# A gated decoder layer: the gates' sigmoids and VectorE's step on them, issued one product later and pinned in their queues

## The chip, the core and the metric

The kernel runs on one core of a Trainium2 chip. The metric is device time in microseconds (us) of one execution. The engines named below are TensorE (PE; its weight loads are listed as PEld), VectorE (DVE), ScalarE (ACT), GpSimd (POOL) and SyncE (SP), which issues most of the DMA transfers. SBUF is the on-chip memory, PSUM the banks into which TensorE accumulates.

## The reference

One layer of a decoder with two token mixers in parallel, a sequence of 2048 positions, width 1024, all in float32. What matters here:

```
h = u @ w_in            # u: the modulated input, 2048 x 1024
q, k, v, a_gate, p_in, p_gate, m_a, m_p = split(h)
a = attention(q, k, v) * silu(a_gate);                     a = a @ w_attn_proj
p = (pool(p_in) @ w_pool_mix * pool_scale) * silu(p_gate); p = p @ w_pool_proj
y = sigmoid(m_a) * a + sigmoid(m_p) * p
...                     # y @ w_out, gate, layer norm
```

Four of the eight parts of h are gates, 1024 wide each. All four go through a sigmoid; `a_gate` is multiplied with its sigmoid (silu), `p_gate` with its sigmoid and with `pool_scale`, and `m_a` and `m_p` stay plain sigmoids.

## The kernel before

**Products.** A float32 product is made of three matmuls on high and low parts (`mm3`). Each weight tile must therefore be split first: ScalarE casts it to its high part (`a.copy(by_two(hi), raw)`, L311) and VectorE subtracts that from the tile to get the low part (`low`, L128). For the last quarter of the weights the cast is L318. The names for the outcome of both are `w_set`.

The products are arranged in a scheme with seven products where eight would be needed (Strassen's). A `Quad` stands for two weight tiles by two column halves, so for four output blocks of 128 x 512. Its seven products are called, by the set of inputs that they use, B11 and T1 (in `front`) and T2, B21, T3, B22, T4 (in `back`). Each product is 12 matmuls of 128 x 512. The sums of weights that a quad needs are formed on GpSimd (L279, L283, L284, L289), some additions on results too (L362, of `p5`).

A result comes free in this order, and `q.consume` is called on each:

- (0, 0): PSUM bank `a`, after B21, with no addition;
- (1, 1): `p5`, after T3 and an addition on VectorE (L378);
- (0, 1): `c12`, after B22 and an addition (L386);
- (1, 0): `u2`, after T4 and an addition (L406).

`ring` runs the quads in groups of two (one group has one): for both quads T2 and B21, then T3 and B22 of the first, T3 and B22 of the second, T4 of both, then B11 and T1 of the next group's quads.

**Gates.** `gate_quads(s)` lists for one half `s` of the sequence one quad for keys and values and 16 gate quads, in nine groups. The first half's phase (`first_phase`) runs from about 75 to 460 us and the second half's (`second_phase`) from about 760 to 1080 us. Between them and after them lie attention, and at the end projections and the norm. A gate block is 128 x 512: a sigmoid on ScalarE (L516), for half of the gates one step on VectorE (L518 for silu, L520 with `pool_scale`), and a store of 256 KB to memory. In all there are 128 sigmoids, 64 steps and 128 stores.

**What sets the order.** Instructions written through `nc.scalar`, `nc.vector` and so on are put into their engine's queue by a scheduler, which may move them. Those written through the wrappers `act`, `dve`, `pe`, `pool`, `sp` (class `Ordered`) are pinned: they keep the order of the program among themselves. TensorE's are all pinned. `tick()` is called after each product. It runs what is hooked at that place (loads and splits of other data sets, pooled weights), counts up, and runs what is due: `defer(n, f)` puts `f` down for the n-th `tick` from now. The store of a gate is deferred by 2.

**Work beside the gates.** Hooks in the two phases prepare data for later stages: sums of inputs and their high and low parts (`k_hi` on ScalarE, `k_lo` on VectorE, stored from there), folds of pooled weights (`mr`, `mhi`, `mlo`), and loads. The transposed weights that are folded with these come through `spare`.

**Buffers.** The sigmoid's tile comes from a pool of five buffers with tag "c", shared with `c12`, `k_hi`, `k_lo`, `vt`, `mr`, `st_hi` and `st_lo`; whoever takes a buffer waits for the one before to be done with it, the landing of its store included. `u2` and `p5` share four buffers with tag "p". PSUM banks with tag "mm" are four.

Of the kernel before, what the change touches and what calls it, by code (L numbers as in the profile page):

```python
# [13 lines left out]
AF = mybir.ActivationFunctionType  # L14
ALU = mybir.AluOpType
# [43 lines left out]
def kernel(  # L59
# [22 lines left out]
    nc = tc.nc  # L82
    pe, act, dve, pool, sp = (Ordered(tc, e) for e in (nc.tensor, nc.scalar, nc.vector, nc.gpsimd, nc.sync))
# [13 lines left out]
    psc = cp.tile([P, KT], F32, name="psc")  # L97
# [23 lines left out]
    gates_d = {n: dp.tile([2, KT, 2, P, CH], F32, name=f"{n}_d") for n in ("ag", "pg", "ma", "mp")}  # L121
# [289 lines left out]
    def defer(ticks, f):  # L411
        due.append((now[0] + ticks, len(due), f))
# [99 lines left out]

    def gate_quad(s, name, base, m, kind):
        def consume(ph, mi, t, src):
            g = ph.c("sig")
            nc.scalar.activation(g, src, AF.Sigmoid)  # L516
            if kind == "silu":
                nc.vector.tensor_tensor(g, g, src, ALU.mult)  # L518
            elif kind == "scaled":
                nc.vector.scalar_tensor_tensor(g, src, psc[:, m + mi : m + mi + 1], g, ALU.mult, ALU.mult)  # L520
            defer(2, lambda: sp.dma_start(gates_d[name][s, m + mi, t], g))

        return Quad((win[base + m], win[base + m + 1]), consume)

# [847 lines left out]
```

## Time and profile before

| what | us |
|---|---|
| three runs | 1878.24, 1870.00, 1867.99 |
| median | 1870.0 |
| profiled execution | 1861.84 |
| its span in the profile | 1860.1 |
| TensorE busy in the span | 1735.2 |
| VectorE busy | 1315.5 |
| ScalarE busy | 938.5 |
| GpSimd busy | 935.5 |

The profiled execution is a fourth one; its own time is 1.7 us above its span. Rows of the profile give an engine, the line of the program that issued the work, the operation and its tiles (out<-in, by the names in the program). In the timeline a row begins with its start and its length in us, and ends in brackets with the idle time of the engine before it and with what ended that. Rows of waits give the engine and line that waited, what it waited for, the total in us, the count and the longest. Rows of a tile's view give the shortest, median and longest duration in ns, then the first and last start in us.

### The profile page before, as it was taken

What the parts mean: (1) busy time and instruction counts of PE and PEld (TensorE: products, weight loads), DVE (VectorE), ACT (ScalarE), POOL (GpSimd) and SP (SyncE); (2) the same over time, 40 slices, a digit from 0 to 9 for tenths busy, and PEclk for the clock granted to TensorE, in tenths of its full rate; (3) what the DMA queues carried; (4) which work ended last, traced back from release to release, by engine and by line L of the source; (5) the groups of instructions that cost most, each with busy time, mean ns of one, the idle gap of its engine ahead of it and who ended that gap; (6) DMA issues with size and microseconds to landing.
All of it is one profiled execution on the core that took longest, in us unless ns stands there. A gap on an engine that the chain in (4) does not pass through costs nothing. (4 is left out here: it accounts for less than half of the span.)

```text
span 1860.1 us, 25320 instructions
## 1 busy us (share of the span) xinstructions
PE 1735.2 (93%) x8248; PEld 1436.4 (77%) x8248; DVE 1315.5 (71%) x2284; ACT 938.5 (50%) x1977; POOL 935.5 (50%) x758
## 2 busy tenths in 40 slices
PE   6689899989999999999999999999989989999996
PEld 6467777777888888787777788888867778777775
DVE  5776766544677787777666457777857887886886
ACT  3543434333777776544444457777724333422453
POOL 0454445433254677545445314556763785476543
PEclk9889999999999999999999999999999999999998
DMA  9245566766344447785777733544786574689432
GB/s 346 74 163 189 198 218 213 254 211 180 107 144 163 159 154 294 262 285 196 254 258 251 259 126 120 181 145 139 278 300 204 185 258 155 214 291 382 146 140 104
DMA packets 163571, 381.32 MB, mean 205 GB/s; under 512 B 19680, under 2 KB 23792, under 8 KB 163440
## 3 DMA queue, kind: packets, MB, share of 16 engines
q1 hardware_dynamic: 150560, 342.95, 52.9%
q0 software_dynamic: 10112, 33.06, 5.2%
q10 hardware_dynamic: 2768, 3.70, 0.9%
q8 instruction: 65, 1.06, 0.2%
q14 instruction: 66, 0.54, 0.1%
HBM read 244.35 MB, written 138.44 MB: 206 GB/s over the span
## 5 line engine op out<-in xcount | busy, mean ns | idle before, releaser
L55 PE MATMUL mm<-set_B,w_set 128*128 128x512 f32 x3240 | 804.1, 396 | 31.7 <-DVE w_set L128 24.3
L55 PEld LDWEIGHTS mm<-set_B,w_set 128*128 128x128 f32 x3240 | 602.2, 189 | 165.8 <-DVE w_set L128 33.5
L55 PE MATMUL lg<-set_T,w_set 128*128 128x512 f32 x2088 | 529.1, 403 | 61.9 <-ACT w_set L311 24.6
L55 PEld LDWEIGHTS lg<-set_T,w_set 128*128 128x128 f32 x2088 | 398.6, 193 | 168.9 <-ACT w_set L311 33.2
L128 DVE TENSOR_TENSOR w_set<-W,w_set 128x1024 fp32r<-128x1024 f32 x162 | 241.4, 1490 | 142.4 <-ACT w_set L311 137.2
L311 ACT CAST w_set<-W 128x1024 fp32r<-128x1024 f32 x162 | 169.3, 1049 | 239.0 <-PE mm L55 146.8
L55 PE MATMUL mm<-set_T,w_set 128*128 128x512 f32 x1080 | 269.0, 397 | 0.6 <-ACT set_T L55 0.3
L55 PEld LDWEIGHTS mm<-set_T,w_set 128*128 128x128 f32 x1080 | 202.3, 190 | 44.6 <-ACT set_T L55 1.5
L289 POOL TENSOR_TENSOR W<-W 128x512 f32<-128x512 f32 x56 | 81.3, 1451 | 158.5 <-DVE w_set L128 149.4
L283 POOL TENSOR_TENSOR W<-W 128x512 f32<-128x512 f32 x56 | 86.8, 1550 | 130.8 <-DVE w_set L128 114.4
L362 POOL TENSOR_TENSOR p<-p,u 128x512 f32<-128x512 f32 x58 | 98.8, 1705 | 104.5 <-DVE u L361 102.2
L55 DVE TENSOR_TENSOR o<-pv,o 64x128 f32<-64x128 f32 x256 | 72.4, 283 | 92.7 <-ACT o L55 89.9
L55 ACT ACTIVATE L<-L,nm 128x257 f32<-128x257 f32 (+1 forms) x256 | 127.2, 498 | 8.6 <-DVE nm L55 3.5
L55 DVE TENSOR_TENSOR k_lo<-spare,k_hi 128x512 fp32r<-128x512 f32 x88 | 90.0, 1029 | 47.0 <-ACT k_hi L55 14.8
L279 POOL TENSOR_TENSOR W<-W,A 128x512 f32<-128x512 f32 x56 | 83.8, 1496 | 74.9 <-DMA W<-in_win_dram 17.0
L55 DVE CUSTOM_DVE_ANT_0 L<-lg,bt,nsink 128x256 f32<-128x256 f32 (+1 forms) x256 | 111.6, 473 | 5.3 <-PE lg L55 1.3
L284 POOL TENSOR_TENSOR W<-W 128x512 f32<-128x512 f32 x56 | 90.0, 1607 | 13.4 <-DMA W<-in_win_dram 10.5
L55 POOL TENSOR_TENSOR w_set<-W,w_set 128x1024 fp32r<-128x1024 f32 x14 | 33.6, 2403 | 122.5 <-ACT w_set L55 89.6
L55 POOL TENSOR_TENSOR p<-nxt,pg 128x512 f32<-128x512 f32 x32 | 41.3, 1291 | 104.0 <-DVE sm L55 103.9
L55 ACT COPY o<-pv 64x256 f32<-64x256 f32 x128 | 47.2, 369 | 82.4 <-PE pv L55 80.3
L55 DVE TENSOR_TENSOR ptl<-pt,pth 128x512 fp32r<-128x512 f32 (+1 forms) x128 | 85.7, 670 | 1.7 <-ACT pth L55 1.6
L55 PE MATMUL lg<-kk,qs 128*128 128x256 f32 (+1 forms) x512 | 80.5, 279 | 0.0
(201 smaller groups left out, 2495.9 us busy)
## 6 DMA issues: line engine op xcount, KB each, us to landing
W<-in_win_dram SPq DMA_DIRECT2D x68, 256.0 KB, 3.7
w_set<-wmix_d SPq DMA_DIRECT2D x32, 512.0 KB, 5.3
A<-in_win_dram SPq DMA_DIRECT2D x34, 256.0 KB, 4.1
W<-in_win_dram POOLq DMA_DIRECT2D x34, 256.0 KB, 3.7
ag_d<-sig SPq DMA_DIRECT2D x32, 256.0 KB, 2.8
pg_d<-sig SPq DMA_DIRECT2D x32, 256.0 KB, 3.7
ma_d<-sig SPq DMA_DIRECT2D x32, 256.0 KB, 3.8
mp_d<-sig SPq DMA_DIRECT2D x32, 256.0 KB, 3.2
```

The lines of the kernel that those rows point to most:

```text
L55: return lambda *args, **kw: self.tc.keep_in_program_order(op(*args, **kw))
L128: engine.tensor_tensor(dst, src, as32(hi), ALU.subtract)
L279: e.tensor_tensor(self.w[:, 1, :], self.w[:, 2, :], self.a22, ALU.add)
L283: e.tensor_tensor(x[:, 1, :], x[:, 1, :], x[:, 0, :], ALU.subtract)
L284: e.tensor_tensor(x[:, 2, :], x[:, 0, :], x[:, 2, :], ALU.subtract)
L289: e.tensor_tensor(x[:, 0, :], x[:, 0, :], x[:, 1, :], ALU.subtract)
L311: a.copy(by_two(hi), raw)
L362: nc.gpsimd.tensor_tensor(p5, p5, u2, ALU.add)
```

## The change

`consume` of `gate_quad` no longer issues the sigmoid, the step on VectorE and the deferred store at once. It puts all three into a function `work` that runs at the next `tick`, so one product later; the store, deferred by 2 from there, comes three ticks after the addition and not two. The sigmoid and VectorE's step are now written through `act` and `dve`, so they are pinned in their queues. The tile is also taken from the pool one product later. Nothing else differs; later lines of the file have numbers higher by 3.

```
     def gate_quad(s, name, base, m, kind):
         def consume(ph, mi, t, src):
-            g = ph.c("sig")
-            nc.scalar.activation(g, src, AF.Sigmoid)
-            if kind == "silu":
-                nc.vector.tensor_tensor(g, g, src, ALU.mult)
-            elif kind == "scaled":
-                nc.vector.scalar_tensor_tensor(g, src, psc[:, m + mi : m + mi + 1], g, ALU.mult, ALU.mult)
-            defer(2, lambda: sp.dma_start(gates_d[name][s, m + mi, t], g))
+            def work():
+                g = ph.c("sig")
+                act.activation(g, src, AF.Sigmoid)
+                if kind == "silu":
+                    dve.tensor_tensor(g, g, src, ALU.mult)
+                elif kind == "scaled":
+                    dve.scalar_tensor_tensor(g, src, psc[:, m + mi : m + mi + 1], g, ALU.mult, ALU.mult)
+                defer(2, lambda: sp.dma_start(gates_d[name][s, m + mi, t], g))
+
+            defer(1, work)
 
         return Quad((win[base + m], win[base + m + 1]), consume)
```

## Prediction

> **What bounds the kernel now.** I read the page first, for the shares of the span; then the busy time by stretch of the two stages in which gate products run; then what TensorE waited for there; then the queues of ScalarE and VectorE, where the change is.
>
> ```profile
> span 1860.1 us, 25320 instructions
> PE 1735.2 (93%) x8248; PEld 1436.4 (77%) x8248; DVE 1315.5 (71%) x2284; ACT 938.5 (50%) x1977; POOL 935.5 (50%) x758
> ```
>
> TensorE is busy 93% of the span, so a step on another engine is worth something only where it makes TensorE wait. The stretches of the two gate stages (75 to 460 and 760 to 1080 us, nine rows, the first and the sum shown; after the comma comes the length, then busy time and count of each engine, the granted clock, the DMA share and GB/s):
>
> ```profile
> core 0: us, PE busy (x) PEld busy (x) DVE busy (x) ACT busy (x) POOL busy (x), PEclk, DMA share, GB/s
> 75.00:130.00 55.00, 42.37 (x163) 32.45 (x162) 44.18 (x53) 25.27 (x40) 36.91 (x51) 0.91 0.49 178
> ...
> sum 705.00, PE 654.42 PEld 527.73 DVE 452.09 ACT 293.98 POOL 328.90; mean PE 72.71 PEld 58.64 DVE 50.23 ACT 32.66 POOL 36.54
> ```
>
> Of 705.00 us TensorE works 654.42. The other 50.6 us (2.7% of the span) are the ceiling of what better order beside the gates can bring, and a quarter of them (55.00 - 42.37 = 12.6) lie in the first 55 us, where the stage fills. What TensorE waited for, first stage above the dots, second below:
>
> ```profile
> PE lg L55 <- ACT w_set L311: 16.3, 9, 4.8
> PE lg L55 <- DVE w_set L128: 8.6, 11, 2.2
> PE mm L55 <- DVE w_set L128: 7.3, 7, 1.3
> PE mm L55 <- DVE set_B L55: 2.8, 1, 2.8
> ...
> PE lg L55 <- DVE w_set L128: 3.5, 6, 1.0
> PE lg L55 <- ACT w_set L311: 3.4, 4, 2.5
> PE mm L55 <- DVE w_set L128: 2.5, 2, 1.4
> ```
>
> Nearly all are waits for a weight tile to be split: L311 is ScalarE's cast to its high part, L128 VectorE's low part. None is a wait for a PSUM bank, which a sigmoid reading it could hold. So the question is which of these two steps stands behind a sigmoid, or behind VectorE's step on one. ScalarE's queue, by what ended its idle time before each step:
>
> ```profile
> ACT sig L516 <- DVE p L378: 47.8, 17, 5.2
> ...
> ACT sig L516 <- DVE c L386: 25.3, 15, 4.3
> ACT sig L516 <- DVE u L406: 25.1, 18, 4.0
> ...
> ACT mhi L55 <- DMA mr<-in_mix_dram: 7.1, 3, 3.5
> ...
> ACT w_set L55 <- DMA spare<-in_wpt_dram: 6.0, 4, 2.5
> ```
>
> ScalarE stood 98.2 us with a sigmoid at its head whose addition was not there yet. That is idle time of an engine at 50%; it costs only where a late cast is queued behind it.
>
> **The change, part by part.** An undisturbed run of TensorE, ten matmuls of the twelve of a product; then three groups of the sigmoids and of VectorE's steps on them, and the landing of the stores:
>
> ```profile
> 293.75 2.47 PE L55 MATMUL mm<-set_B,w_set 128*128 128x512 f32 x10
> ```
>
> ```profile
> L516 ACT ACTIVATE sig<-p x32: 624/632/636, 101.9 to 1067.1; 128x512 f32<-128x512 f32 x32
> ...
> L518 DVE TENSOR_TENSOR sig<-sig,mm x8: 672/678/689, 78.1 to 829.2; 128x512 f32<-128x512 f32 x8
> ...
> L518 DVE TENSOR_TENSOR sig<-sig,u x8: 679/1086/2256, 115.0 to 852.7; 128x512 f32<-128x512 f32 x8
> ...
> DMA to landing us min/median/max: 2.0/3.4/11.4
> ```
>
> *Nothing is added or removed.* 128 sigmoids of 0.63 us, 64 steps on VectorE and 128 stores move back by one product: 12 matmuls, at 2.47 us for ten some 2.9. Work in those engines is equal; only the order counts.
>
> *How far they really move.* The scheduler had already set some later work ahead of the sigmoids. Comparing the two orders of instructions, a sigmoid stands on the average only 0.6 places further back on ScalarE (128 of them, 80 places in all) and VectorE's step one place; only 6 places in all are won by the L311 casts on ScalarE, and the order of TensorE and GpSimd is the same but for two or three swaps. So most of the 98.2 us will turn into idle time in front of something else.
>
> *The long L311 waits: nothing.* In the first stage the large ones stand where pooled weights are folded in:
>
> ```profile
> 127.34 1.22 PE L55 MATMUL lg<-set_T,w_set 128*128 128x512 f32 x2 [4.82 <-ACT w_set L311]
> ...
> 312.99 0.73 PE L55 MATMUL lg<-set_T,w_set 128*128 128x512 f32 x2 [1.58 <-ACT w_set L311]
> 314.25 4.12 PE L55 MATMUL lg<-set_T,w_set 128*128 128x512 f32 x10 [0.53 <-DVE w_set L128]
> ...
> 394.30 0.73 PE L55 MATMUL lg<-set_T,w_set 128*128 128x512 f32 x2 [3.42 <-ACT w_set L311]
> ```
>
> ScalarE comes late to these because the steps before the cast wait for loads (7.1 and 6.0 us in its rows, from mr and spare). The sigmoids stand behind the cast already. I take 0, between 0 and -1.6 (the one at 312.99 gone).
>
> After such a wait ten matmuls take 4.12 us, where ten undisturbed take 2.47: a wait of 2.1 us in two parts costs 1.65 us more. The Trainium skill, "TensorE: Matmul & The Clock Gate", section "What's actually happening", says that the clock is halved after an idle window of about 3.4 us, with windows that run freely. By it a wait of 2.1 us alone should not slow what follows; in the row it does, and I go by the row.
>
> *The short waits at a group's start: a gain.* Where TensorE goes from the last T4 to the next group's B11, VectorE must have split the second quad's first tile:
>
> ```profile
> 107.61 1.65 PE L55 MATMUL mm<-set_B,w_set 128*128 128x512 f32 x6 [0.76 <-DVE w_set L128]
> ...
> 207.25 2.11 PE L55 MATMUL mm<-set_B,w_set 128*128 128x512 f32 x8 [0.98 <-DVE w_set L128]
> ...
> 300.69 1.66 PE L55 MATMUL mm<-set_B,w_set 128*128 128x512 f32 x6 [1.29 <-DVE w_set L128]
> ...
> 857.32 1.88 PE L55 MATMUL mm<-set_B,w_set 128*128 128x512 f32 x7 [1.11 <-DVE w_set L128]
> ```
>
> ```profile
> 201.62 2.15 DVE L518 TENSOR_TENSOR sig<-sig,u 128x512 f32<-128x512 f32 x1
> 203.69 1.77 DVE L55 TENSOR_TENSOR k_lo<-spare,k_hi 128x512 fp32r<-128x512 f32 x1
> ...
> 205.99 1.21 DVE L128 TENSOR_TENSOR w_set<-W,w_set 128x1024 fp32r<-128x1024 f32 x1
> ```
>
> ```profile
> 201.91 3.00 POOL L55 TENSOR_TENSOR spare<-spare 128x512 f32<-128x512 f32 x2
> ```
>
> Ahead of that split stands a step on a sigmoid that takes 2.15 us while GpSimd works beside it, three times the 0.68 of its kind from PSUM. In the changed order this step stands behind the split. The four waits add up to 0.76 + 0.98 + 1.29 + 1.11 = 4.14 us. Bounds 0 and -4.1; I take -3.5, as the k_lo ahead of the split stays and may now be the one that stretches.
>
> On the stretch: the Trainium skill, "SBUF — State Buffer", section "Who interferes with whom", says that a VectorE instruction with two SBUF inputs contends with GpSimd for an exclusively locked port pair, and that one with at most one does not. The trace agrees: up to 2256 ns with two SBUF inputs, at most 689 with one in PSUM. By that rule alone the moved steps would stretch wherever they land, which speaks against a gain.
>
> *The "c" ring in the second stage: a cost.* Sigmoids and the sums c12 (L386) take turns in five buffers. In the changed program the second quad's c12 waits in 9 places for the landing of the store of the first quad's sigmoid of p5, which is issued in the same product. Before, 7 such waits reach one or two products back. And the split that stood ahead of c12 can stand behind it:
>
> ```profile
> 889.69 1.23 DVE L128 TENSOR_TENSOR w_set<-W,w_set 128x1024 fp32r<-128x1024 f32 x1
> 890.84 0.68 DVE L386 TENSOR_TENSOR c<-mm,u 128x512 f32<-128x512 f32 x1
> ```
>
> ```profile
> 891.09 2.20 PE L55 MATMUL mm<-set_B,w_set 128*128 128x512 f32 x9
> ```
>
> TensorE begins on that tile as the split ends. A late c12 there passes 1:1 into the wait. What a wait for a landing costs VectorE is seen once, before:
>
> ```profile
> DVE c L386 <- DMA mp_d<-sig: 3.9, 1, 3.9
> ```
>
> A landing of 3.4 us at the median less a product of 2.9 leaves 0.5 a place. With four groups in each stage: first stage 0 to 2, taken as 0.5 (there the split mostly stays ahead of c12); second 0 to 6 (1.5 a place), taken as 1.6.
>
> *Stores.* They come one product later on SP's queue, so that later loads move ahead of some of them, and whoever takes the buffer waits longer. The row for what this can cost:
>
> ```profile
> 899.64 0.49 SPq L55 DMA_DIRECT2D pg_d<-sig  x1
> ```
>
> ```profile
> 905.61 0.62 ACT L55 CAST k_hi<-spare 128x512 fp32r<-128x512 f32 x1 [3.29 <-DMA pg_d<-sig]
> ```
>
> This landing (issue to the cast that it released: 6.0 us) held ScalarE for 3.29 us. In the changed program k_hi stands 59 places earlier in all, so the waiting is the same or shifts. I take 0, between -2 and +3.3. At the start the 2.8 us wait on set_B grows by half a sigmoid, +0.3.
>
> **Sum:** -3.5 + 0.5 + 1.6 + 0.3 = -1.1 us, 1861.84 to 1860.7 for the profiled execution, whose span is 1860.1. Its time is 8.2 us below the median of the runs, 1870.0, so the median goes to 1868.9. The three runs differ by 10.3 us among themselves; 0.5%, or 9.35 us, is about what a measurement can tell from no change. Adding the ends gives -7.7 (1.6 + 4.1 + 2 gained) to +11.6 (2 + 6 + 3.3 + 0.3 lost and nothing gained), so 1862 to 1882.
>
> **The rivals.** *The sigmoids do block the casts.* For: 98.2 us of ScalarE's idle time ends with their additions. Then most of TensorE's waits on L311 go, 16.3 + 3.4 = 19.7, and the short ones, 4.1: -23.8, or 1846. Half of it gives 1858. Against: only 6 places are won by these casts, and the large waits follow loads. Chance 0.17 for more than 9.35 us.
>
> *The landing of a store decides, and it is slower.* One mechanism: c12 of the second quad waits on VectorE for a store that was issued a product later than before, and the split for TensorE's next product stands behind c12. It decides from 2.3 us a place (4 x 2.3 = 9.35), which is a landing of 5.2 us against the product of 2.9. At 6.0 us, as in the row at 899.64, a place costs 3.1, and 1.65 more for the slowed matmuls: 4.7. Four groups in the second stage make +19, 1889. For: the split at 889.69 has no slack. Against: a median landing of 3.4. Chance 0.20 for more than 9.35 us.
>
> *It does nothing.* The scheduler had placed most casts ahead already, the two-input steps stretch beside GpSimd wherever they stand, and gain and loss are each under 1 us: 1870. Chance 0.20; with the forecast's own 0.43 this makes the 0.63 within 0.5%.
>
> **How the numbers follow.** Forecast 0.43, nothing 0.20, gain 0.17, loss 0.20. The range takes in the forecast's ends and a part of the gain (to -14) and of the loss (to +14): 1856 to 1884, with 0.08 of the gain and 0.10 of the loss outside. Faster 0.17, same 0.63, slower 0.20. Likeliest 1868.9.
>
> **What would show it.** Right: the waits at the group starts near 107, 207, 300 and 857 us fall below 0.3; the waits on L311 at 127, 313 and 394 stay within 0.5; the idle time of ScalarE that ends with an addition falls well under 98 and another's grows; TensorE's idle sum over the two stages stays at 49 to 52. Wrong to the fast side: L311 waits under 10 us. Wrong to the slow side: c12 waits on landings of sigmoid stores in several groups after 760 us, and TensorE on L128 right behind them; or TensorE waits at places that have none now.

## The result and the profile after

The changed kernel is slower: 1872.45 us at the median of 20 runs, against 1866.17 for the kernel before, also 20 runs. The ratio is 1.003, with a 95% interval of 1.0018 to 1.0042; 0.3% of 1866 is 5.6 us. The prediction had 1868.9 against 1870.0 for its three runs, a ratio of 0.9994, so it had the wrong sign. The loss is under the 0.5% that the prediction called the bound of measuring with three runs; twenty runs make that bound smaller. The first lines of the profile after:

```profile
span 1865.6 us, 25317 instructions
PE 1739.6 (93%) x8248; PEld 1438.3 (77%) x8248; DVE 1309.3 (70%) x2284; ACT 943.5 (51%) x1977; POOL 934.7 (50%) x758
```

The engines do the same work. What TensorE waited for in the first gate stage (75 to 470 us):

```profile
PE lg L55 <- ACT w_set L311: 22.3, 10, 8.2
PE lg L55 <- DVE w_set L128: 5.8, 10, 0.9
PE mm L55 <- DVE w_set L128: 4.9, 5, 1.4
PE mm L55 <- DVE set_B L55: 2.8, 1, 2.8
PE mm L55 <- ACT w_set L311: 1.8, 2, 1.1
```

Two things changed at once. TensorE's waits on VectorE's split L128 fell, from 8.6 + 7.3 to 5.8 + 4.9. The waits on ScalarE's cast L311, which were to stay at 16.3, rose to 22.3. ScalarE's own waits, from its whole list and then from that of 75 to 465 us:

```profile
ACT sig L55 <- DVE p L378: 29.1, 11, 4.5
...
ACT sig L55 <- DVE u L406: 19.3, 14, 2.3
...
ACT sig L55 <- DVE c L386: 17.3, 10, 3.5
```

```profile
ACT sig L55 <- DMA wmix_d<-st_hi: 10.8, 7, 2.8
ACT sig L55 <- DMA wmix_d<-st_lo: 9.5, 2, 5.1
```

The idle time in front of sigmoids that waited for their additions fell from 98.2 to 65.7 us. But sigmoids now wait longer for landings. `wmix_d<-st_hi` and `wmix_d<-st_lo` are the stores of a fold's result, from buffers of the "c" ring (the pool of five with that tag); sigmoids waited 2.1 and 5.6 us for them before. Added over all rows of ScalarE's waits between 75 and 465 us that end with the landing of a store from that ring, it was 27.0 us in 12 waits before and is 44.3 in 27 now.

TensorE's instructions stand in the same order in both kernels, 8248 of them. So the same matmul can be found in every trace, and the time from one matmul to another compared. From the 176th to the 1800th (62 to 470 us before) most stretches of 24 matmuls agree to 0.02 us. The largest difference that comes back unchanged in other runs stands at the second half of the first fold. ScalarE there, before and after:

```profile
136.33 0.59 ACT L1012 CAST st_hi<-pt 128x512 fp32r<-128x512 f32 x1 [0.85 <-PE pt L55]
136.81 1.06 ACT L55 CAST w_set<-spare 128x1024 fp32r<-128x1024 f32 x1
138.90 1.05 ACT L311 CAST w_set<-W 128x1024 fp32r<-128x1024 f32 x1 [1.03 <-issue]
139.85 0.58 ACT L609 CAST vv<-pt 128x512 fp32r<-128x512 f32 x1
140.32 0.60 ACT L516 ACTIVATE sig<-mm 128x512 f32<-128x512 f32 x1
```

```profile
138.10 0.59 ACT L1015 CAST st_hi<-pt 128x512 fp32r<-128x512 f32 x1 [0.85 <-PE pt L55]
140.25 0.60 ACT L55 ACTIVATE sig<-mm 128x512 f32<-128x512 f32 x1 [1.56 <-DMA wmix_d<-st_hi]
140.74 1.04 ACT L55 CAST w_set<-spare 128x1024 fp32r<-128x1024 f32 x1
141.68 0.59 ACT L612 CAST vv<-pt 128x512 fp32r<-128x512 f32 x1
142.16 1.06 ACT L311 CAST w_set<-W 128x1024 fp32r<-128x1024 f32 x1
```

Before, a sigmoid stood behind both casts. Now one stands ahead of both, and waits 1.56 us until a store of the fold's first half has landed and its buffer is free. It is not the same one (that of 140.32 now runs at 153.30), but the one that ran at 124.24 us before. TensorE at that place, before and after:

```profile
140.00 0.73 PE L55 MATMUL lg<-set_T,w_set 128*128 128x512 f32 x2 [0.51 <-ACT w_set L311]
141.25 2.60 PE L55 MATMUL lg<-set_T,w_set 128*128 128x512 f32 x10 [0.52 <-DVE w_set L128]
```

```profile
143.27 0.73 PE L55 MATMUL lg<-set_T,w_set 128*128 128x512 f32 x2 [2.02 <-ACT w_set L311]
144.89 4.14 PE L55 MATMUL lg<-set_T,w_set 128*128 128x512 f32 x10 [0.90 <-DVE w_set L128]
```

The first wait grew by 1.51 us, the second by 0.38, and the ten matmuls behind them by 1.54: 3.43 us in all. The 24 matmuls around this place, from the ninth of the product before it on, took 6.20 us before (137.97 to 144.17) and take 9.60 now.

### The profile page after: what moved, and what is told of

The parts are those of the page before. It is cut to its first block, busy times and chain, and to the rows that moved or that the text cites. A ratio compares the mean times of both kernels' runs of the same rounds, so it can differ in the third digit from the quotient of the medians.

```text
span 1865.6 us, 25317 instructions
## 1 busy us (share of the span) xinstructions
PE 1739.6 (93%) x8248; PEld 1438.3 (77%) x8248; DVE 1309.3 (70%) x2284; ACT 943.5 (51%) x1977; POOL 934.7 (50%) x758
## 5 line engine op out<-in xcount | busy, mean ns | idle before, releaser
L128 DVE TENSOR_TENSOR w_set<-W,w_set 128x1024 fp32r<-128x1024 f32 x162 | 237.3, 1465 | 135.3 <-ACT w_set L311 129.1
L311 ACT CAST w_set<-W 128x1024 fp32r<-128x1024 f32 x162 | 169.7, 1050 | 218.1 <-PE mm L55 133.4
L55 ACT CAST k_hi<-spare 128x512 fp32r<-128x512 f32 x88 | 54.1, 620 | 74.1 <-POOL spare L55 26.9
```

Of the source, the lines that this page charges most:

```text
L55: return lambda *args, **kw: self.tc.keep_in_program_order(op(*args, **kw))
L128: engine.tensor_tensor(dst, src, as32(hi), ALU.subtract)
```

## The experiments

Theory A: sigmoids that come later stand in ScalarE's queue ahead of casts that TensorE needs, and wait there for a buffer of the ring. Theory B: pinning costs. Rival C: many small losses, in both stages. Rival D: the late additions' sigmoids are the cause, not those of (0, 0). In the table, "first" and "second" are the times of the 24 matmuls around the start of the first and of the second half of the first fold, in us, and "ring" is ScalarE's waits for ring stores, summed as above. Ratios are to the kernel before, run beside each. All kernels but the one before, before_c6, before_tables and delay_only have the sigmoids and VectorE's steps pinned.

| kernel | ratio (95% interval) | first | second | ring |
|---|---|---|---|---|
| before | 1 | 12.30 | 6.20 | 27.0 |
| changed | 1.003 (1.0018 to 1.0042) | 15.48 | 9.60 | 44.3 |
| pin_only | 1.0001 (0.9987 to 1.0014) | 12.58 | 6.17 | 20.5 |
| delay_only | 1.0033 (1.0020 to 1.0046) | 14.23 | 9.59 | 47.0 |
| first_only | 1.0036 (1.0019 to 1.0053) | 14.44 | 9.59 | 42.7 |
| second_only | 1.0003 (0.9990 to 1.0017) | 13.13 | 6.17 | 19.4 |
| mm_at_once | 0.9988 (0.9973 to 1.0004) | 12.52 | 6.15 | 32.0 |
| mm_only | 1.0042 (1.0027 to 1.0057) | 11.58 | 9.59 | 43.3 |
| one_late | 1.0024 (1.0005 to 1.0043) | 11.90 | 10.07 | 31.3 |
| one_at_once | 1.0010 (0.9994 to 1.0027) | 14.39 | 6.20 | 46.1 |
| early_tile | 1.0020 (1.0005 to 1.0035) | 15.52 | 9.59 | 47.8 |
| before_c6 | 0.9954 (0.9934 to 0.9974) | 11.22 | 6.17 | 15.0 |
| after_c6 | 0.9955 (0.9939 to 0.9971) | 12.44 | 6.17 | 24.7 |
| mm_at_once_c6 | 0.9942 (0.9921 to 0.9963) | 9.42 | 6.16 | 21.3 |
| before_tables | 0.9980 (0.9961 to 0.9999) | 11.66 | 6.16 | 27.3 |
| after_tables | 1.0012 (0.9993 to 1.0030) | 14.17 | 9.59 | 47.0 |

### Pin or delay

pin_only keeps everything at once and pins it:

```
-            nc.scalar.activation(g, src, AF.Sigmoid)
+            act.activation(g, src, AF.Sigmoid)
...          # nc.vector -> dve likewise
```

> The sigmoid and VectorE's step are pinned but issued at once, as before. The order of instructions on all five engines comes out the same as before, waits included. Theory A (buffer ring: the loss comes from the later place of the sigmoids, which then wait in ScalarE's queue for buffers of the c ring): ratio 1.000, within 0.997 and 1.003, TensorE's waits on L311 in the first stage near 17 us. Theory B (pinning as such costs): ratio near 1.003.

delay_only is the change with `nc.scalar` and `nc.vector` inside `work`.

> Issued one product later, not pinned. The order on the engines differs from the changed kernel in about ten places. Theory A: as the changed kernel, ratio 1.002 to 1.004, waits of TensorE on L311 in the first stage 20 us or more, ScalarE's waits for landings of ring stores in the first stage near 44 us (27.0 before). Theory B: ratio 1.000.

Measured: 1.0001 and 1.0033. Theory B falls: the pinned kernel has the same order on every engine as the kernel before, so the scheduler had kept these instructions in the program's order anyway. The delay alone makes the loss.

### One stage or both

```
-            defer(1, work)
+            if s == 0:          # second_only: s == 1
+                defer(1, work)
+            else:
+                work()
```

> Only the first gate stage (75 to 460 us) has the later sigmoids. From the two traces TensorE is 5.4 us late at the start of attention of the first half (739.13 to 744.51) and gains back 1.9 by the end of the second stage's attention. Theory A with the fold casts as the place: ratio 1.0025 to 1.0035 (+5 to +6.5 us). Rival C (the loss is spread over both stages, wherever c12 waits for a store): ratio 1.001 to 1.002.

> Only the second gate stage (760 to 1080 us) has the later sigmoids. Theory A with the fold casts, which are only in the first stage: ratio 0.998 to 1.000 (0 to -3 us). Rival C: ratio 1.001 to 1.002, with TensorE waiting on L128 behind c12 after 760 us.

Measured: 1.0036 and 1.0003. The loss lies in the first stage, where the folds are. So Rival C in its form of both stages falls. Of the waits of c12 in the second stage, which the prediction had priced at 1.6 us, nothing is seen; the interval of second_only would allow up to 3.2.

### Which results

mm_at_once issues the sigmoid of (0, 0) at once and delays the other three. mm_only is the reverse.

```
-            defer(1, work)
+            if (mi, t) == (0, 0):
+                work()
+            else:
+                defer(1, work)
```

> As changed, but the result (0, 0), which needs no addition, gets its sigmoid at once; the other three come one product later. In the changed kernel this sigmoid stands ahead of the cast of the second half of the first fold on ScalarE (140.25 us, after 1.56 us of waiting for the landing of a store of the fold's result), and 24 matmuls there take 9.6 us where they took 6.2 before. Theory A (the late sigmoids stand ahead of casts and wait there for buffers of the c ring): this stretch goes back to 6.2 us and the ratio falls to 1.000 to 1.002 (3.4 of 5.6 us gone). Rival D (it is the later stores and steps of the three with an addition): ratio stays at 1.003.

> Only the result (0, 0), which needs no addition, has its sigmoid a product later, the other three at once: the other half of the run that had (0, 0) at once (ratio 0.9988). Theory A: second half of the first fold 9.6 us, ratio 1.002 to 1.004. Rival (the loss needs the later p5, c12 and u2 as well): ratio 1.000.

Measured: 0.9988, the interval just holding 1, and 1.0042. The result that needs no addition is the one whose delay costs; with it at once, nothing is lost (1.000 to 1.002 was expected). Rival D falls.

### One sigmoid of 128

one_late has the order of the kernel before, with the single sigmoid of the rows above issued one product later. one_at_once is the changed kernel with this one alone issued at once.

```
-            defer(1, work)
+            if (s, name, m, mi, t) == (0, "ag", 2, 0, 0):   # one_late
+                defer(1, work)
+            else:
+                work()
```

> The kernel before with one sigmoid of 128 issued a product later: that of the result (0, 0) of the quad beginning at weight tile 2 of attn_gate, first half, which stands beside the first fold. In the changed kernel it is the one at 140.25 us, ahead of the fold's second cast. Theory A (that place on ScalarE is what costs): 24 matmuls of the second half of the first fold go from 6.2 to 9.6 us, ratio 1.001 to 1.003. Rival C (the loss is a sum over many places): those matmuls stay near 6.2 or the ratio stays at 1.000.

> The changed kernel with this one sigmoid alone issued at once. Theory A: 24 matmuls of the second half of the first fold back at 6.2 us, the 24 of its first half (12.3 to 13.1 before, 14.2 to 15.5 in the changed forms) stay late, as the chain of buffers ahead of it is unchanged; ratio 1.000 to 1.002. Rival C: ratio 1.003.

Measured: 1.0024 and 1.0010. One sigmoid moved makes the second half of the fold late by 3.9 us (10.07 against 6.20), and 0.24% is 4.5 us (interval 1 to 8 us). Its rows in one_late, ScalarE and TensorE:

```profile
135.89 0.59 ACT L1018 CAST st_hi<-pt 128x512 fp32r<-128x512 f32 x1 [0.85 <-PE pt L55]
138.03 0.60 ACT L55 ACTIVATE sig<-mm 128x512 f32<-128x512 f32 x1 [1.55 <-DMA wmix_d<-st_hi]
138.52 1.04 ACT L55 CAST w_set<-spare 128x1024 fp32r<-128x1024 f32 x1
```

```profile
141.53 0.74 PE L55 MATMUL lg<-set_T,w_set 128*128 128x512 f32 x2 [2.49 <-ACT w_set L311]
143.26 4.03 PE L55 MATMUL lg<-set_T,w_set 128*128 128x512 f32 x10 [1.00 <-DVE w_set L128]
```

The same wait of 1.55 us, with no other sigmoid moved. In the first half of the fold (column "first") one_at_once stays late, as expected.

### Order of the ring or more buffers

early_tile takes the buffer at the addition and delays the rest:

```
+            g = ph.c("sig")
+
             def work():
-                g = ph.c("sig")
```

> As changed, but the sigmoid's buffer is taken at the addition, so that the c ring turns in the order of before, while sigmoid, step and store come one product later. Theory A with the order of the ring as cause: ratio 1.000 to 1.001, ScalarE's waits for landings of ring stores in the first stage back towards 27 us (44.3 as changed). Theory A with the place of the sigmoids in the queue as cause: ratio 1.002 to 1.004.

Measured: 1.0020, and 47.8 us of waits. The sigmoid waits for the same store as in the changed kernel:

```profile
140.10 0.60 ACT L55 ACTIVATE sig<-mm 128x512 f32<-128x512 f32 x1 [1.54 <-DMA wmix_d<-st_hi]
```

A buffer given out at the addition, ahead of the fold's, could not wait for a store of that fold. So taking the tile earlier in the program did not bring back the old order of the ring, and this run does not tell the order of the ring from the place in the queue. The runs with six buffers separate the wait for the buffer from the place.

after_c6 and before_c6 have six buffers in the first stage. To make room, the tables `carry` and `fix` of the pooling are placed after that stage (the edit is shortened here).

```
-    carry = cp.tile([P, KT, 16], F32, name="carry")
...                                  # fix likewise; both are set up after this stage
-    with Pools("g0", spare=2, p=4, c=5) as ph:
+    with Pools("g0", spare=2, p=4, c=6) as ph:
```

> As changed, with six buffers in the c ring of the first stage where five were (two small tables of the pooling are placed after that stage to make room). Theory A: ScalarE's waits for landings in the first stage fall well under 44 us, the 24 matmuls of the second half of the first fold go from 9.6 back to about 6.2 us, ratio 0.998 to 1.001. Rival (position in the queue alone, no matter which buffer): ratio 1.003.

> The kernel before with six buffers in the c ring of the first stage: what the sixth buffer gives without the change. Theory A: the kernel before waited 27 us there on ScalarE, of which little reached TensorE, so ratio 0.997 to 1.000.

> The changed kernel with the two tables placed after the first stage and still five buffers in the c ring: the control for six buffers. If the sixth buffer took the loss away: ratio 1.002 to 1.004, as changed, and 9.6 us for the 24 matmuls of the second half of the first fold. If the moved tables did: ratio 0.995 to 0.997 and 6.2 us.

> The kernel before with the two tables moved and five buffers. If the sixth buffer gave the gain of 0.46%: ratio 0.999 to 1.001. If the moved tables did: 0.995 to 0.997.

Measured: 0.9955 and 0.9954, both faster than expected; with six buffers the change costs nothing that these intervals of some 0.2% show. The last two are the control with the tables moved and five buffers: 1.0012 and 0.9980. The move alone brings about 0.2%, which was not expected, but it leaves the change's loss as it was (1.0012 / 0.9980 = 1.0032). Against these controls the sixth buffer brings 0.57% to the changed kernel (0.9955 / 1.0012, intervals apart) and 0.26% to the one before (0.9954 / 0.9980), where the intervals overlap, so that this gain is not shown. ScalarE in after_c6:

```profile
135.66 0.59 ACT L1008 CAST st_hi<-pt 128x512 fp32r<-128x512 f32 x1 [0.85 <-PE pt L55]
136.14 0.60 ACT L55 ACTIVATE sig<-mm 128x512 f32<-128x512 f32 x1
136.63 1.05 ACT L55 CAST w_set<-spare 128x1024 fp32r<-128x1024 f32 x1
138.22 1.05 ACT L309 CAST w_set<-W 128x1024 fp32r<-128x1024 f32 x1 [0.54 <-issue]
```

This run tells apart what one_late could not: the sigmoid stands at the same place, ahead of both casts, but has its buffer at once, and the stretch takes 6.17 us. The place itself costs 0.6 us of ScalarE's time, which the idle time ahead of the next cast takes in; the wait for the buffer costs TensorE the 3.4 us.

The Trainium skill, "Perfetto Trace Analysis", section "Identifying Performance Opportunities", says that gaps which keep coming back on the engine that should be saturated can mean too few buffers for the next tile. The runs agree: with the sixth buffer ScalarE's waits for ring stores fell from 44.3 to 24.7 us (47.0 in the control with five), and TensorE's on ScalarE's cast in the first stage from 22.3 to 14.2 (22.0 in the control).

mm_at_once_c6 joins the two that were best.

> (0, 0) at once, the other three a product later, six buffers in the c ring of the first stage: the two that were fastest, together. If the ring is the only cause, the sixth buffer has taken all that there is and the ratio is that of six buffers alone, 0.994 to 0.997; if the place in the queue adds to it, 0.992 to 0.994.

Measured: 0.9942 (0.9921 to 0.9963), 1858.5 us at the median of 6 runs. It beats both kernels. Against six buffers alone (0.9954) the intervals overlap, so the earlier (0, 0) adds nothing that is shown.

## Why the prediction was wrong

**The step that failed is "The long L311 waits: nothing".** It took 0, with 0 to -1.6 as bounds, because the sigmoids "stand behind the cast already". The sign for it was that the waits at 127, 313 and 394 us stay within 0.5. They went from 4.82, 1.58 and 3.42 us to 8.22, 3.44 and 1.89, and the one at the second half of the first fold from 0.51 to 2.02. At this last place, which the prediction does not list, the changed order puts a sigmoid ahead of the cast, and this was to be seen in the order of instructions before any run. It is a sigmoid that before did not stand behind the cast either: it ran ahead of the cast of the fold's first half (124.24 in the rows below), where the cast waited for its load anyway. The runs show 3.4 to 3.9 us there in each of the seven kernels that delay that sigmoid with five buffers (9.59 to 10.07), and none in the nine others (6.15 to 6.20).

**At the first half of the first fold a chain of waits for the ring came later.** ScalarE ahead of the cast, before and after:

```profile
113.07 0.63 ACT L516 ACTIVATE sig<-u 128x512 f32<-128x512 f32 x1 [1.74 <-DMA ag_d<-sig]
...
120.94 0.62 ACT L55 CAST k_hi<-spare 128x512 fp32r<-128x512 f32 x1 [2.11 <-DMA u_T_split<-k_hi]
...
124.24 0.60 ACT L516 ACTIVATE sig<-mm 128x512 f32<-128x512 f32 x1
125.29 1.04 ACT L55 CAST w_set<-spare 128x1024 fp32r<-128x1024 f32 x1 [0.46 <-DMA spare<-in_wpt_dram]
126.24 1.04 ACT L311 CAST w_set<-W 128x1024 fp32r<-128x1024 f32 x1
```

```profile
115.82 0.63 ACT L55 ACTIVATE sig<-u 128x512 f32<-128x512 f32 x1 [1.70 <-DMA u_T_split<-k_hi]
...
122.83 0.62 ACT L55 CAST k_hi<-spare 128x512 fp32r<-128x512 f32 x1 [2.61 <-DMA u_T_split<-k_hi]
...
128.22 1.04 ACT L311 CAST w_set<-W 128x1024 fp32r<-128x1024 f32 x1
```

The chain begins 2.8 us later, at the sigmoid of u2, and the cast comes 2.0 us later. (TensorE is at the fold 1.4 us earlier, which is the rest of the growth from 4.82 to 8.22.) The 72 matmuls from 106 to 134 us take 28.9 to 30.9 us in the six kernels with five buffers that delay the first stage's results (one_at_once, which delays all but one, included), and 27.2 to 28.0 in the five that have nearly the order of before there (before, pin_only, second_only, before_tables and one_late). Which link of the chain makes the difference was not tried.

**The "c" ring was the right resource with the wrong waiter.** The prediction looked at c12 on VectorE, priced it in the second stage (+1.6) and gave the first stage +0.5. second_only shows no loss that can be measured. The waiter that mattered most is the sigmoid on ScalarE, in the first stage, and what it waits for is not a store of a gate but one of a fold. The term of +0.3 for the start was nothing: the wait on `set_B` is 2.8 us in both. So the slower rival (0.20) had the mechanism, a late landing through the ring that holds a split which TensorE needs, but the wrong store, engine and stage. Its cost was 5.6 us where it priced 19.

**The short waits at a group's start came out in two places of four.** At 207 and 300 us the waits are gone: 24 matmuls there take 5.44 us each after 6.73 and 7.03, a gain of 2.9 us. TensorE at both, without a wait, then VectorE ahead of the first, in the changed kernel:

```profile
213.12 2.88 PE L55 MATMUL mm<-set_B,w_set 128*128 128x512 f32 x12
...
306.97 2.88 PE L55 MATMUL mm<-set_B,w_set 128*128 128x512 f32 x12
```

```profile
211.77 1.21 DVE L128 TENSOR_TENSOR w_set<-W,w_set 128x1024 fp32r<-128x1024 f32 x1
212.90 0.68 DVE L55 TENSOR_TENSOR sig<-sig,u 128x512 f32<-128x512 f32 x1
213.50 1.77 DVE L55 SCALAR_TENSOR_TENSOR sig<-u,psc,sig 128x512 f32<-128x512 f32 x1
```

The split is ahead of the steps on sigmoids, as forecast. At the two others the waits stayed:

```profile
107.21 2.59 PE L55 MATMUL mm<-set_B,w_set 128*128 128x512 f32 x10 [1.01 <-DVE w_set L128]
...
859.75 2.57 PE L55 MATMUL mm<-set_B,w_set 128*128 128x512 f32 x10 [0.99 <-DVE w_set L128]
```

They were 0.76 and 1.11. And of the 2.9 us the 1.6 at 300 us is not kept. In the six kernels TensorE gets to the third fold 12.9 to 13.3 us after the matmul at 297 us, in the five 14.4 to 14.8; but the cast that it waits for there ends at 15.9 to 17.3 us in the six and at 15.7 to 17.1 in the five. So the wait at the fold, 1.58 us before, takes back what the group start gave:

```profile
321.46 0.73 PE L55 MATMUL lg<-set_T,w_set 128*128 128x512 f32 x2 [3.44 <-ACT w_set L311]
```

That leaves 1.3 us of the 3.5: the term was mis-sized by 2.2, as it did not ask what TensorE waits for next.

**The stretched steps moved rather than went away.** VectorE's steps on p5, in the first row as they were before, now take longer, and those on u2 less:

```profile
L518 DVE TENSOR_TENSOR sig<-sig,p x8: 680/691/1743, 105.1 to 839.1; 128x512 f32<-128x512 f32 x8
...
L55 DVE TENSOR_TENSOR sig<-sig,p x8: 686/1390/1780, 107.1 to 841.8; 128x512 f32<-128x512 f32 x8
...
L55 DVE TENSOR_TENSOR sig<-sig,u x8: 674/681/1961, 116.5 to 857.9; 128x512 f32<-128x512 f32 x8
```

The median on p5 rose from 691 to 1390 ns, that on u2 fell from 1086 to 681. By the rule on shared ports that the prediction drew from the Trainium skill ("SBUF — State Buffer", "Who interferes with whom"), steps with two SBUF inputs contend with GpSimd's reads wherever they land. The trace agrees: of the eight steps on p5, the five that took 1220 to 1780 ns each had at least 1.1 us of GpSimd's work beside them, and the three at 686 to 693 ns had none.

**What stays open.** The loss adds up only roughly, as single profiled executions differ by several us among themselves: 3.4 us at the second half of the first fold, about 2.4 up to its first half (the means of the six and of the five), less 1.3 at 207 us, so some 4.5 of the 5.6. The column "first" holds waits that also depend on when TensorE arrives. The half stays late, at 14.39, when the one sigmoid is at once, and is 12.52 when all of (0, 0) are and 11.58 when only they are late; what makes it late is open. Nor is it shown why the two tables, moved, bring 0.2%.

**A sign that misled.** The prediction named TensorE's idle time in fixed windows, 49 to 52 us, as a sign of being right. It came out so, with a loss of 5 us beside it:

```profile
sum 705.00, PE 653.37 PEld 525.63 DVE 450.19 ACT 297.36 POOL 329.67; mean PE 72.60 PEld 58.40 DVE 50.02 ACT 33.04 POOL 36.63
```

That is 51.6 us idle, 1.0 more than before. In the later kernel the same windows hold other instructions, and slow matmuls count as busy. Matmul by matmul the loss was plain.

## What to carry to other kernels

Before an instruction is moved later, look at which buffer it will ask for at its new place and whose store must land first, at every place where it comes to stand ahead of a cast that the busiest engine needs: one sigmoid of 128, moved alone, cost 0.24%, where all of them cost 0.30%. Delay only what has something to wait for; the quarter of the results that needs no addition carried the cost. When a move costs through a ring of buffers, one more buffer may be worth more than any order: here it took away the loss, and both kernels with six buffers are 0.45% faster than the kernel before, about 0.2% of which came with the tables that were moved to make room.

## What the runs showed of the hardware

Two short waits close together slowed what followed. At the same matmuls, in before and after (window of the ten matmuls with the two ahead of them; the clock is the column after POOL):

```profile
139.90:144.00 4.10, 3.48 (x15) 2.60 (x16) 2.52 (x5) 1.03 (x3) 0.00 (x0) 1.00 0.56 186
```

```profile
143.20:149.00 5.80, 4.84 (x14) 3.54 (x15) 1.64 (x3) 0.01 (x1) 0.00 (x0) 0.71 0.40 136
```

With waits of 0.51 and 0.52 us the granted clock stays at 1.00; with 2.02 and 0.90 it is 0.71 over the stretch, and ten matmuls take 4.14 us for 2.60. Nearly half of the 3.43 us lost there is this. In finer windows of the changed kernel:

```profile
141.66:145.07 3.41, 0.91 (x3) 0.48 (x4) 3.02 (x4) 1.55 (x3) 0.00 (x0) 1.00 0.19 67
145.07:148.48 3.41, 3.41 (x9) 2.63 (x10) 0.00 (x0) 0.00 (x0) 0.00 (x0) 0.50 0.67 225
```

So the clock fell to half for 3.41 us, right behind 3.41 us in which TensorE was busy for only 0.91, though never idle for longer than 2.02 at a time. In these sixteen traces the clock changes on such a grid of 3.41 us. Between 75 and 465 us they hold 1666 of these steps at full clock: all 95 in which TensorE was busy for less than 0.44 of the step were followed by one at half clock, none of the 1518 above 0.58, and 13 of the 53 between.
